# Layer 1 of a diffusion step: other turns at the passage into it, and another order of weights, gate and tiles at its end

## The chip, the cores and the metric

The kernel runs on one core of a Trainium2 chip. The metric is the device time of one launch in microseconds (us), median of several runs. The engines named are TensorE (PE; PEld is its weight load), VectorE (DVE), ScalarE (ACT), GpSimd (POOL) and SyncE (SP). SP and POOL issue nearly all DMAs, each through a queue of its own.

## The reference, cut to what matters

There are 640 tokens (512 of the sample, 128 of the context, which is the fifth tile of 128 tokens and is modulated by rows of its own), a model width of 1024 and two layers. Layer 0 is attention with a gated MLP beside it, layer 1 is centred pooling; each is followed by a squared-ReLU MLP of width 4096. All arithmetic that counts is float32.

```python
def squared_relu_mlp(h, w1, w2):
    a = jax.nn.relu(h @ w1)
    return (a * a) @ w2

# pooling mixer of layer 1: group g has the window w of (2, 4, 8, 16)
mean = (cs[:, end, sl] - cs[:, start, sl]) / cnt          # centred mean over w tokens
outs.append((mean - h32[..., sl]) @ w_pool[gi])

# every sub-layer: RMSNorm -> shift, scale -> mixer or MLP -> gate -> residual add
# at the end: y = rms_norm(x, final_g)
```

## The kernel before, in words

**Products.** A float32 product is made of three fast ones (fp32r): each operand is split into a high and a low part, and lines 823, 824 and 825 issue high by high, high by low, and low by high. For a weight the high part is a copy on ScalarE (L213). Its low part is made in one of two ways: VectorE subtracts the high part from the raw weight (L223, "VectorE makes the low part"), or ScalarE writes the negative high part (L216) and a GpSimd DMA adds the raw weight to it from memory (L220). In both cases L825, or L824 where the weight is the moving operand, has to wait for the low part.

**The stream of weights.** `st` holds a list of items, one for each piece of a weight, in the order in which they are used. `st.pump(n)` takes the next n: it issues loads on SP while raw tiles are free, and writes ScalarE's copy; the low part by VectorE is put into `lag` and written at once (`lows()`), except while `st.lagging` is set: then it is written at the next `pump` or `need`. `st.need(key)` pumps until a weight is there. `st.lo = None` selects the way over ScalarE and the DMA. So the places of `pump` in the program decide where a weight's passes stand in the engines' queues.

**MLP.** The 640 tokens go in two chunks (columns) of 320, or 328 and 312 in layer 0. In `mlp`, block b of 512 of the 4096 inner columns has four up tiles (`up_ps`, over eight parts of h, `h0` to `h7`) and then the down product (`dn_ps`). The square-ReLU of an up tile is L1502 to L1506: VectorE (`r`), ScalarE, VectorE (`aa`). In layer 0's last two blocks the down products of the second chunk are added to x for d = 0 to 7; `per_d0` squares each result for the norm.

**The passage from layer 0 to layer 1.** When seven eighths of the second chunk are done, `tick0` calls `pool_mm(0, …)`: the pooling's product for the first chunk, its residual adds (L1429), squares (L714, L729), the sum over partitions (`R_ps`, L740), an rsqrt on 128x3 values (L663 to L668, tile nrm5), its spread over the columns (L684) and then h (generator `g0`: L766 on VectorE, L770 on ScalarE, L774 on VectorE for each of eight parts). Between the squares `pool_mm` pumps a weight of block 0 of layer 1, `w1(1,0,·)`. The second chunk's pooling (generator `g1`: products `pt` L1903, `hh` L1907, windows `win` L1945, differences `dif` L1981) is interleaved with this. The string table `TURNS` says in what order, one entry at each up tile: '0' a step of g0, '1' a step of g1, 'w' a weight by ScalarE and the DMA, 'W' a weight by VectorE.

**The end.** Layer 1's last block has two more up tiles that are made with seven products of sums instead of eight (`up7`, `product`: L1632 u2, u3, r on VectorE). The output is computed with tokens as rows: tile t of 128 tokens, half q of 512 columns, in the order `LASTS = 4, 3, 2, 0, 1` (4 is the context). The sum over the earlier blocks, y, is multiplied by the gate's row (L2032; G for the context is row 1, for the others row 0), x is added to it by a GpSimd DMA from `xT` (L2033), and the last block's product comes in by gy = ps·G (L2042) and y + gy (L2043). Then follow the product with final_g (L2059), the rsqrt and the output. The context's tile takes another way: its last product is added to y first (L1738), and then the gate is applied. Row 0 of the gate is loaded by SP (L2020) just ahead of the last `up7`, row 1 and final_g behind it.

Of the kernel before, what the change touches and what calls it, by code (L numbers as in the profile page):

```python
# [45 lines left out]
H512 = slice(0, 512)  # L46
TAIL = slice(0, 256), slice(256, 512)
PARKS = 0, 1, 4, 3, 2
PARK_AT = {(0, 4): 1, (0, 5): 1, (0, 6): 1, (0, 7): 1, (1, 4): 1, (1, 5): 2, (1, 6): 2, (1, 7): 1}
# [5 lines left out]
STEPS = (4,) * 8  # L55
TURNS = '11w', 'w', '10', 'w01', '0w1', '01110', '11W11', '1', 'w0101', 'w1', '', '1', '', '11111', '111', '', '0w'
VM_LAG = 3, 4
# [74 lines left out]
class Weights:  # L132
# [3 lines left out]
    def __init__(self, nc, raw):  # L136
        self.nc, self.raw = nc, raw
        self.items, self.loaded, self.done = [], 0, 0
        self.raw_live, self.raw_cap, self.tiles, self.of = 0, RAWB, {}, {}
        self.raws = {}  # L140
        self.slots = None
        self.caps = {}

        self.lo = nc.vector
        self.own = {}
        self.hold = None
        self.slow = ()
        self.later, self.skip = [], False
        self.keep, self.second = {}, None
        self.lag, self.lagging = [], False  # L150
# [40 lines left out]
    def pump(self, n=1):  # L191
# [4 lines left out]
        while n > 0 and self.done < len(self.items):  # L196
# [9 lines left out]
            if use is None:  # L206
                if own is None:
                    self.of[key], w = self.slots.take([128, 2, 1024], F32R)
                else:
                    w = own()  # L210
                r = ts[0][:, 0:size]
                hi, lo = w[:, 0, 0:size], w[:, 1, 0:size]
                self.nc.scalar.activation(out=hi, in_=r, func=AF.Copy)  # L213
                eng = None if key[0] in self.slow else self.lo
                if eng is None:
                    self.nc.scalar.activation(out=lo, in_=hi.bitcast(F32), func=AF.Copy, scale=-1.0)  # L216
                    src, shape = loads[0]
                    if len(shape) == 2:
                        lo = lo.rearrange("p (k n) -> p k n", k=shape[0])
                    self.nc.gpsimd.dma_start(out=lo, in_=src, accum_op=ALU.add)  # L220
                else:
                    self.lag.append(
                        lambda: eng.tensor_tensor(out=lo, in0=r, in1=hi.bitcast(F32), op=ALU.subtract)  # L223
                    )
                self.tiles[key] = w
                rest = None
            else:
                rest = use(ts)
# [58 lines left out]
def body(ctx, tc, a):  # L287
# [303 lines left out]
    def add_w1s(l, b):  # L591
        for p in range(FB // 2):
            src = [(rows(a["w_ff1"][l], k, 4, b * 512 + p * 256, 256), (4, 256)) for k in (0, 4)]
            for i in range(7):
                key = ("w1s", l, b, p, i)
                st.add(key, [] if i else src, 0, w1s_use(l, b, p, i))
                st.keep[key] = 2 if i == 6 else 0

    def add_w2h(l, b):
        for i in range(4):  # L600
            for k, h in [(i // 2 * 2, i % 2) if b == NFB - 1 else (i % 2 * 2, i // 2)]:
                st.add(("w2", l, b, k, h), [(rows(a["w_ff2"][l], b * FB + k, 2, h * 512, 512), (2, 512))], 1024)

    def add_w2(l, b):
        for k in range(FB):
            r = (b * FB + k) * 128
            st.add(("w2", l, b, k), [(a["w_ff2"][l, r:r + 128, :], (1024,))], 1024)

    add_w1(0, 0)
    vm = vmods(1)  # L610
    for b in range(1, NFB + 1):
        n0 = len(st.items)
        if b < NFB:
            add_w1(0, b)
        add_w2(0, b - 1)
        ws, st.items[n0:] = st.items[n0:], []
# [8 lines left out]
    for b in range(NFB):  # L625
        if b >= 2:
            add_w1s(1, b)
        add_w2h(1, b)

# [839 lines left out]
    def mlp(l, C, H, lead, CL, per_d, per_c, mid, tick=None, turn=None, seven=False):  # L1469
# [58 lines left out]
        def down(b, d, c, ps=None, last=True, ks=range(FB)):  # L1528
# [3 lines left out]
            for j, k in enumerate(ks):  # L1532
                if seven:
                    w, v = st.need(("w2", l, b, k - k % 2, d // 4)), k % 2 * 4 + d % 4
# [60 lines left out]
        def up7(b, p, last=False):  # L1595
            n = C[0][1]
            gates = [(t, q) for t in LASTS[1:] for q in range(2)] if last else []

# [53 lines left out]
            pd = product(1, 2, None, True)  # L1652
            st.pump()
            pb = product(2, 1, None, True)
# [29 lines left out]
        def blocks7(f0):  # L1684

            st.lagging = True
            for b in range(NFB):
                if b >= f0:
                    for p in range(FB // 2):
                        if b == NFB - 1 and p:  # L1690
                            gate_load(0, rawp.tile([128, 1024], F32, tag="raw", name="G"))
                        up7(b, p, b == NFB - 1 and p == 1)
# [27 lines left out]

                todo = [(t, q) for t in LASTS for q in range(2)]
                st.pump(4)
                early = cut(todo[0:4])
# [5 lines left out]
                zs += [st.slots.take([128, 2, 1024], F32)[1].rearrange("p a n -> p (a n)") for _ in range(2)]  # L1729
                cell["zs"] = [z[:, 0:1024] for z in zs]  # L1730
                for t, q in todo:
                    i = LASTS.index(t)
                    for v in TAIL if (t, q) == todo[-1] else (H512,):
                        ps = early.pop((t, q), None)
                        ps = down_t(b, t, q, v, ps, True, range(FB) if ps is None else (3, 2))
                        if not i:
                            y = tile_q(t, q)
                            vec.tensor_tensor(out=y, in0=cols(ps), in1=y, op=ALU.add)  # L1738
                            last_gate(t, (q,))
                        else:  # L1740
                            last_more(t, q, v, ps)
                            last_sq(t, q, v, q + (v.start > 0))
                    if q and i == 2:

                        for k in range(2):
                            last_sq(LASTS[0], k, H512, k)
                        last_out(LASTS[0:3], False)
                    elif q and i > 2:
                        last_out(LASTS[i:i + 1], i == 4)

# [73 lines left out]
        while f2 < NFB:  # L1824
# [10 lines left out]
            if tick and f2 == NFB - 2:  # L1835
                for c, sizes in zip(C, AHEAD):
                    d0 = 0
                    for n in sizes:
# [5 lines left out]
                        if c is C[1] and d0 + n == KD:  # L1844
                            for k in range(FB):
                                st.free(("w2", l, f2, k))
                        tick(c, d0)
                        for d in range(d0, d0 + n):
                            residual(down(f2 + 1, d, c, pss[d - d0]), d, c, modc[l, 5])
                            per_d(c, d)  # L1850
                        d0 += n
                    per_c(c)
                for k in range(FB):
                    st.free(("w2", l, f2 + 1, k))
                return
# [189 lines left out]
    def last_sq(t, q, v, i):  # L2045
# [3 lines left out]
        if (t, "ss") not in cell:  # L2049
            i3 = LASTS.index(t)  # L2050
            if ("ss", i3 // 3) not in cell:
# [9 lines left out]
    def last_out(ts, both):  # L2061
        i3, n = LASTS.index(ts[0]), len(ts)
        ss = cell["ss", i3 // 3]
# [18 lines left out]
    xT = dr.tile([T, D], F32, name="xT")  # L2082
    grow = dr.tile([2, D], F32, name="grow")
    LASTS = (4, 3, 2, 0, 1)

    def pool_mm(ci, N, gs=POOL_ORDER):
# [3 lines left out]
        for g in gs:  # L2090
            for m in range(2):
# [7 lines left out]
                N.square(2 * g + m)  # L2099
                if ci == 0 and m:  # L2100
                    st.pump()

# [10 lines left out]
    def tick0(c, d):  # L2113
# [7 lines left out]
        keep()  # L2121
        st.lo = None
        st.caps["w1", 1, 0, 0] = RAWB
        N[0] = Norm(x, C1[0], vec)
# [4 lines left out]
    def per_d0(c, d):  # L2129
# [5 lines left out]
        if c == C0[1]:  # L2135
            bg.step(3)
            if d >= POOL_AT:
                st.pump()

# [15 lines left out]
    def turn1(what):  # L2155


        for t in what:
            if t in "01":
                next((g0, g1)[int(t)], None)  # L2160
            else:
                st.lo = None if t == "w" else vec
                st.pump()
                st.lo = vec

    turn1(TURNS[0])

# [103 lines left out]
```

## Time and profile before

| | us |
|---|---|
| median of 3 runs | 1283.76 (1283.36 to 1283.88) |
| the profiled execution | 1285.38 |
| its span (first to last instruction) | 1283.6 |
| TensorE matmul busy | 1247.0 (97%) |
| TensorE weight load busy | 1135.7 (88%) |
| VectorE busy | 796.9 (62%) |
| ScalarE busy | 571.1 (44%) |
| GpSimd busy | 198.5 (15%) |

The mean granted TensorE clock of the profiled execution is 0.988 of 2.4 GHz. Waits, rows and clocks below are from this one execution; its time is 1.6 us above the median. Each row of an instruction has its start, its duration, engine, line, operation, output<-input, and in brackets the idle time of its engine just before it and what ended it.

### The profile page before, as it was taken

How to read it: one execution, taken by the hardware profiler on the slowest of the kernel's cores; microseconds unless marked ns; L12 is line 12 of the kernel's file. 1: busy time of each engine (PE TensorE's matmuls, PEld its weight loads, DVE VectorE, ACT ScalarE, POOL GpSimd, SP SyncE). 2: the span in 40 equal slices, each digit the busy share in tenths (PEclk: the TensorE clock that was granted, in tenths of full speed). 3: DMA queues.
4: the chain of work that ended last, by engine and by line, in shares of the span. 5: the costliest groups of instructions: out<-in, count | busy, mean ns of one | idle time of the engine just before them, and what ended most of it. 6: DMA issues, size and time to landing. Idle time of an engine off the chain costs nothing. (4 is left out here: it accounts for less than half of the span.)

```text
span 1283.6 us, 19571 instructions
## 1 busy us (share of the span) xinstructions
PE 1247.0 (97%) x7744; PEld 1135.7 (88%) x7744; DVE 796.9 (62%) x1455; ACT 571.1 (44%) x1022; POOL 198.5 (15%) x181
## 2 busy tenths in 40 slices
PE   6999999999999999999999999899999999999986
PEld 4899975689999999999999999889898989989875
DVE  5753854554766566666666637775576556675667
ACT  4445654543554434334332424745444515445154
POOL 0010122212122221313131314210000000000030
PEclk9999999999999999999999999899999999999988
DMA  7752696250344443535353441904113343132273
GB/s 297 262 167 68 152 254 235 97 197 1 120 139 139 124 154 119 158 121 159 120 161 118 142 139 29 234 27 128 60 33 100 83 82 96 37 122 76 66 128 102
DMA packets 79163, 161.89 MB, mean 126 GB/s; under 512 B 7728, under 2 KB 34864, under 8 KB 78560
## 3 DMA queue, kind: packets, MB, share of 16 engines
q1 hardware_dynamic: 69296, 145.94, 35.6%
q0 software_dynamic: 9344, 14.35, 6.2%
q8 instruction: 61, 1.00, 0.3%
q10 hardware_dynamic: 432, 0.35, 0.1%
q14 instruction: 30, 0.25, 0.1%
HBM read 149.46 MB, written 8.02 MB: 123 GB/s over the span
## 5 line engine op out<-in xcount | busy, mean ns | idle before, releaser
L823 PE MATMUL up_ps<-h,w 128*128 128x320 f32 (+2 forms) x800 | 251.8, 315 | 4.7 <-DVE r L1632 3.1
L824 PE MATMUL up_ps<-h,w 128*128 128x320 f32 (+2 forms) x800 | 249.4, 312 | 1.2 <-DVE h L774 1.2
L825 PE MATMUL up_ps<-h,w 128*128 128x320 f32 (+2 forms) x800 | 249.9, 312 | 0.0
L213 ACT ACTIVATE w<-raw 128x1024 fp32r<-128x1024 f32 (+4 forms) x131 | 132.8, 1027 | 109.6 <-DMA raw<-w_ff 84.1
L223 DVE TENSOR_TENSOR w<-raw,w 128x1024 fp32r<-128x1024 f32 (+4 forms) x122 | 151.5, 1249 | 48.0 <-ACT w L213 47.1
L823 PEld LDWEIGHTS up_ps<-h,w 128*128 128x128 f32 x800 | 152.4, 190 | 9.1 <-issue 6.7
L823 PE MATMUL dn_ps<-aa,w 128*128 128x328 f32 (+1 forms) x512 | 159.1, 311 | 0.0
L824 PE MATMUL dn_ps<-aa,w 128*128 128x328 f32 (+1 forms) x512 | 159.0, 311 | 0.0
L825 PE MATMUL dn_ps<-aa,w 128*128 128x328 f32 (+1 forms) x512 | 158.1, 309 | 0.0
L824 PEld LDWEIGHTS up_ps<-h,w 128*128 128x128 f32 x800 | 152.7, 191 | 1.9 <-DVE h L774 1.6
L825 PEld LDWEIGHTS up_ps<-h,w 128*128 128x128 f32 x800 | 152.2, 190 | 0.3 <-DMA w<-w_ff 0.3
L484 POOL TENSOR_TENSOR acc<-acc,raw 128x1024 f32<-128x1024 f32 x42 | 100.7, 2397 | 303.7 <-ACT raw L482 303.7
L824 PE MATMUL dn_ps<-w,aa 128*128 128x512 f32 (+1 forms) x324 | 126.1, 389 | 2.4 <-DVE w L223 2.4
L823 PE MATMUL dn_ps<-w,aa 128*128 128x512 f32 (+1 forms) x324 | 126.8, 391 | 0.0
L825 PE MATMUL dn_ps<-w,aa 128*128 128x512 f32 (+1 forms) x324 | 126.3, 390 | 0.0
L1429 DVE SCALAR_TENSOR_TENSOR x<-dn_ps,mod,x 128x328 f32<-128x328 f32 (+2 forms) x168 | 67.3, 435 | 68.0 <-PE dn_ps L825 67.3
L576 ACT ACTIVATE w<-raw 128x512 fp32r<-128x512 f32 x84 | 51.0, 625 | 120.5 <-DVE raw L583 120.5
L823 PEld LDWEIGHTS dn_ps<-aa,w 128*128 128x128 f32 x512 | 96.4, 188 | 1.8 <-ACT r L1502 0.8
L825 PEld LDWEIGHTS dn_ps<-aa,w 128*128 128x128 f32 x512 | 96.3, 188 | 0.0
L824 PEld LDWEIGHTS dn_ps<-aa,w 128*128 128x128 f32 x512 | 96.2, 188 | 0.1
L482 ACT ACTIVATE raw<-raw,cs 128x1024 f32<-128x1024 f32 x42 | 48.3, 1150 | 62.5 <-DVE acc L477 58.0
L824 PEld LDWEIGHTS dn_ps<-w,aa 128*128 128x128 f32 x324 | 61.3, 189 | 15.5 <-DVE w L223 2.8
(403 smaller groups left out, 2421.1 us busy)
## 6 DMA issues: line engine op xcount, KB each, us to landing
raw<-w_ff SPq DMA_DIRECT2D x126, 512.0 KB, 3.8
raw<-w_mod SPq DMA_DIRECT2D x80, 512.0 KB, 3.9
raw<-w_m SPq DMA_DIRECT2D x16, 512.0 KB, 6.5
raw<-w_out SPq DMA_DIRECT2D x8, 512.0 KB, 4.5
w<-w_ff POOLq DMA_DIRECT2D x8, 512.0 KB, 9.8
kT<-ckvT POOLq DMA_DIRECT2D x4, 768.0 KB, 11.0
xr<-x SPq DMA_DIRECT2D x5, 512.0 KB, 6.2
xs<-x SPq DMA_DIRECT2D x2, 1280.0 KB, 10.1
```

The costliest lines, as they stand in the source:

```text
L213: self.nc.scalar.activation(out=hi, in_=r, func=AF.Copy)
L223: lambda: eng.tensor_tensor(out=lo, in0=r, in1=hi.bitcast(F32), op=ALU.subtract)
L482: act(out=raw if k else acc[1], in_=raw, func=AF.Copy, scale=w[1])
L484: nc.gpsimd.tensor_tensor(out=acc[1], in0=acc[1], in1=raw, op=ALU.add)
L576: act(out=w[:, 0], in_=src, func=AF.Copy)
L823: mm(ps, lhsT=st_[0], rhs=mv[0], start=first, stop=False, skip_group_check=on)
L824: mm(ps, lhsT=st_[0], rhs=mv[1], start=False, stop=False, skip_group_check=on)
L825: mm(ps, lhsT=st_[1], rhs=mv[0], start=False, stop=last, skip_group_check=on)
L1429: vec.scalar_tensor_tensor(out=xv, in0=ps[:, p0:p0 + c1 - c0], scalar=gate[:, d, m:m + 1], in1=xv, op0=ALU.mult, op1=ALU.add)
```

## The change

Five things are changed; the matmuls and their order on TensorE are the same.

1. The last two `w_ff2` blocks of layer 0 are loaded in halves (two k by 512 columns), so that half of their slots come free at d = 3. The four weights `w1(1,0,·)` are then made at d = 3, 4 and 5 in `per_d0`, and `pool_mm` no longer pumps.
2. `TURNS` is written anew: the first chunk's h (0) stands ahead, and one weight is made over ScalarE and the DMA ('w') and three by VectorE ('W'), where before there were four 'w' ahead of the first 'W'. `st.lagging` is set before the first turn instead of later.
3. Row 0 of the gate is an item of the weights' stream, and stays in its raw tile.
4. Two of the last block's `w_ff2` pieces have their low part made by ScalarE and the GpSimd DMA (`st.dma`) instead of by VectorE.
5. The order of tiles at the end is 3, 2, 4, 0, 1 (`ENDS`); the gates of 3, 2 and 0 are applied during the last `up7`, those of 4 and 1 behind it, and tile 4 takes the same way as the others.

```diff
+ENDS = 3, 2, 4, 0, 1
-TURNS = '11w', 'w', '10', 'w01', '0w1', '01110', '11W11', '1', 'w0101', 'w1', '', '1', '', '11111', '111', '', '0w'
+TURNS = '11', '', '01', '0w', '01W', '0W1', '011', '0W1', '11', '11', '11', '11', '1', '11111', '111', '', '0w'
...
-                eng = None if key[0] in self.slow else self.lo
+                eng = None if key[0] in self.slow or key in self.dma else self.lo
...
-        add_w2(0, b - 1)
+        (add_w2h if b > NFB - 2 else add_w2)(0, b - 1)
...
+        if b == NFB - 1:
+            st.add(("gate",), [(grow[0:1, :].to_broadcast([128, D]), (D,))], 0, lambda ts: cell.update({("G", 0): ts[0]}))
+            st.keep["gate",] = 0
+            st.dma = [("w2", 1, b, 0, h) for h in range(2)]
         add_w2h(1, b)
...
-            gates = [(t, q) for t in LASTS[1:] for q in range(2)] if last else []
+            gates = [(t, q) for t in ENDS[0:2] + ENDS[3:4] for q in range(2)] if last else []
...
-            st.pump()
+            st.pump(1 + last)
...
-                        if b == NFB - 1 and p:
-                            gate_load(0, rawp.tile([128, 1024], F32, tag="raw", name="G"))
...
-                st.pump(4)
+                st.pump(5)
+                st.lows()
                 early = cut(todo[0:4])
...
+                last_gate(NT - 1)
+                last_gate(ENDS[-1])
...
-                        if not i:
-                            y = tile_q(t, q)
-                            vec.tensor_tensor(out=y, in0=cols(ps), in1=y, op=ALU.add)
-                            last_gate(t, (q,))
-                        else:
-                            last_more(t, q, v, ps)
-                            last_sq(t, q, v, q + (v.start > 0))
+                        last_more(t, q, v, ps)
+                        last_sq(t, q, v, q + (v.start > 0))
...
+                            if c is C[1] and d == 3:
+                                free2(f2, 0)
+                                free2(f2 + 1, 0)
...
                 N.square(2 * g + m)
-                if ci == 0 and m:
-                    st.pump()
...
-        st.lo = None
-        st.caps["w1", 1, 0, 0] = RAWB
+        st.caps["w1", 1, 0, 2] = RAWB
...
-            if d >= POOL_AT:
-                st.pump()
+            if 3 <= d < POOL_AT:
+                st.lo = None
+                st.pump(2 if d == 3 else 1)
...
+    st.lagging = True
     turn1(TURNS[0])
```

**VectorE's queue at the passage**, around the four square-ReLUs of layer 1's first block, before (numbers behind names are those of buffers; after the change all lines are one to ten higher):

```order
L1981 SCALAR_TENSOR_TENSOR dif2_8225<-win_8223,hh2_8014 128x2x328
L1945 TENSOR_TENSOR win_8241<-hh1_8018 128x2x330
L1503 TENSOR_TENSOR r_8244<-r_8244,up_ps_8052 128x320
L1506 TENSOR_TENSOR aa_8243<-r_8244,aa_8243 128x320
L1503 TENSOR_TENSOR r_8250<-r_8250,up_ps_8053 128x320
L1506 TENSOR_TENSOR aa_8249<-r_8250,aa_8249 128x320
L1945 TENSOR_TENSOR win_8255<-win_8241 128x2x328
L1503 TENSOR_TENSOR r_8258<-r_8258,up_ps_8054 128x320
L1506 TENSOR_TENSOR aa_8257<-r_8258,aa_8257 128x320
L1503 TENSOR_TENSOR r_8264<-r_8264,up_ps_8055 128x320
L1506 TENSOR_TENSOR aa_8263<-r_8264,aa_8263 128x320
L1980 TENSOR_TENSOR win_8255<-win_8255,cnt_3357 128x2x2x8
```

The same place after the change (here L224 is the low part of a weight, L1513 and L1516 the square-ReLU, L1947 a window):

```order
L1983 SCALAR_TENSOR_TENSOR dif2_8243<-win_8235,hh2_8014 128x2x328
L1947 TENSOR_TENSOR win_8247<-hh1_8018 128x2x330
L1513 TENSOR_TENSOR r_8250<-r_8250,up_ps_8044 128x320
L1516 TENSOR_TENSOR aa_8249<-r_8250,aa_8249 128x320
L1947 TENSOR_TENSOR win_8255<-win_8247 128x2x328
L1513 TENSOR_TENSOR r_8258<-r_8258,up_ps_8045 128x320
L1516 TENSOR_TENSOR aa_8257<-r_8258,aa_8257 128x320
L224 TENSOR_TENSOR w_8183<-raw_8083,w_8183 128x1024
L1982 TENSOR_TENSOR win_8255<-win_8255,cnt_3358 128x2x2x8
```

Behind the fourth square-ReLU now stands the low part of w_8183, the third that VectorE makes there; the two others stand further ahead in the queue. TensorE reads w_8183 in the first up tile of block 1.

**GpSimd's queue at the end**, before, the first six of ten alike (x0 and x1 are the two halves of x's columns):

```order
L2033 DMA x0_2778<-xT_3359 128x4x128
L2033 DMA x1_2779<-xT_3359 128x4x128
L2033 DMA x0_2778<-xT_3359 128x4x128
L2033 DMA x1_2779<-xT_3359 128x4x128
L2033 DMA x0_2778<-xT_3359 128x4x128
L2033 DMA x1_2779<-xT_3359 128x4x128
```

After:

```order
L2035 DMA x0_2779<-xT_3360 128x4x128
L2035 DMA x1_2780<-xT_3360 128x4x128
L221 DMA w_11709<-w_ff2 128x2x512
L2035 DMA x0_2779<-xT_3360 128x4x128
L2035 DMA x1_2780<-xT_3360 128x4x128
L221 DMA w_11731<-w_ff2 128x2x512
L2035 DMA x0_2779<-xT_3360 128x4x128
```

Two weights' low parts (L221 adds the raw weight from memory) now stand between the transfers of x, behind those of the first and of the second tile.

**VectorE's queue at the last product of the last `up7`**, before (L581 is the low part of a sum of weights, L2032 a gate, r the row for which a product waits):

```order
L581 TENSOR_TENSOR w_11629<-raw_11384,w_11629 128x512
L1632 TENSOR_TENSOR u2_11701<-p1_11671,up_ps_11688 128x320
L1632 TENSOR_TENSOR u3_11702<-u2_11701,up_ps_11673 128x320
L2032 TENSOR_TENSOR x0_2778<-x0_2778,G_11652 128x4x128
L2032 TENSOR_TENSOR x1_2779<-x1_2779,G_11652 128x4x128
L581 TENSOR_TENSOR w_11629<-raw_11386,w_11629 128x512
L1632 TENSOR_TENSOR r_11657<-u3_11702,up_ps_11714 128x320
```

After:

```order
L582 TENSOR_TENSOR w_11626<-raw_11381,w_11626 128x512
L582 TENSOR_TENSOR w_11626<-raw_11383,w_11626 128x512
L1642 TENSOR_TENSOR u2_11701<-p1_11666,up_ps_11688 128x320
L1642 TENSOR_TENSOR u3_11702<-u2_11701,up_ps_11668 128x320
L2034 TENSOR_TENSOR x0_2779<-x0_2779,raw_11388 128x4x128
L2034 TENSOR_TENSOR x1_2780<-x1_2780,raw_11388 128x4x128
L1642 TENSOR_TENSOR r_11652<-u3_11702,up_ps_11713 128x320
```

The gate reads raw_11388, the raw tile of the stream's gate item, instead of the tile G of a load of its own, and the second L582 has moved ahead of the sums.

## Rows read from the trace of the kernel before

**Rows 1.** Window of the end: start:end, length, busy (count) by engine, clock, DMA, GB/s.
```profile
1200.00:1284.00 84.00, 66.63 (x341) 59.15 (x339) 54.17 (x103) 34.16 (x74) 13.06 (x10) 0.88 0.46 101
```
**Rows 2.** TensorE's waits, whole span: for whom, us in all, times, longest.
```profile
PE up_ps L823 <- DVE r L1632: 3.1, 1, 3.1
...
PE dn_ps L824 <- DVE w L223: 2.4, 1, 2.4
...
PE R_ps L740 <- DVE sq L729: 1.5, 1, 1.5
PE R_ps L684 <- DVE nrm5y L668: 1.4, 1, 1.4
PE up_ps L824 <- DVE h L774: 1.2, 2, 0.9
...
PE up_ps L823 <- DVE r L1503: 0.7, 1, 0.7
```
**Rows 3.** Windows of half clock behind these places, columns as in rows 1.
```profile
810.20:817.03 6.83, 6.83 (x29) 6.83 (x29) 3.85 (x13) 6.09 (x10) 1.47 (x2) 0.50 1.08 261
1233.46:1240.28 6.82, 6.19 (x23) 6.22 (x24) 6.82 (x12) 5.16 (x9) 6.82 (x6) 0.50 0.80 189
1250.52:1253.94 3.42, 3.42 (x10) 2.68 (x9) 1.38 (x2) 0.00 (x0) 0.00 (x0) 0.50 1.29 160
```
**Rows 4.** Timeline of TensorE at the passage: the matmul that reads the third weight's low part.
```profile
833.12 0.41 PE L825 MATMUL up_ps<-h,w 128*128 128x320 f32 x1
```
**Rows 5.** Timeline of ScalarE before and at the passage: idle time, one weight's pass.
```profile
787.88 0.46 ACT L714 ACTIVATE sq<-x 128x312 f32<-128x312 f32 x1 [8.29 <-DVE x L1429]
...
795.11 1.04 ACT L213 ACTIVATE w<-raw 128x1024 fp32r<-128x1024 f32 x1
```
**Rows 6.** VectorE at the passage: two rows of rsqrt, one window, its waits in it.
```profile
806.00 0.18 DVE L665 RECIPROCAL nrm5y<-nrm5y 128x3 f32<-128x3 f32 x1 [0.60 <-ACT nrm5y L664]
806.21 1.73 DVE L666 TENSOR_TENSOR nrm5t<-nrm5y,nrm5v 128x3 f32<-128x3 f32 x1
...
809.37:837.42 28.05, 27.09 (x164) 26.39 (x164) 20.39 (x46) 22.42 (x43) 4.81 (x4) 0.88 0.88 201
...
DVE h L774 <- ACT h L770: 3.7, 3, 2.4
DVE aa L1506 <- ACT aa L1505: 2.2, 4, 0.5
DVE ht L766 <- ACT hh L1907: 1.1, 1, 1.1
```
**Rows 7.** Timeline of VectorE behind the passage: a weight's low part and its next row.
```profile
875.58 1.23 DVE L223 TENSOR_TENSOR w<-raw,w 128x1024 fp32r<-128x1024 f32 x1 [0.46 <-ACT w L213]
876.72 0.48 DVE L1503 TENSOR_TENSOR r<-r,up_ps 128x320 f32<-128x320 f32 x1
```
**Rows 8.** GpSimd's DMAs: weights at 780:840 (first), x at 1220:1284 (second), x's issues.
```profile
DMA to landing us min/median/max: 6.2/9.8/11.2
...
DMA to landing us min/median/max: 4.6/10.6/11.7
...
1232.96 10.47 POOL L2033 DMA_DIRECT2D x<-xT  x8 [380.77 <-DVE x L2032]
```
**Rows 9.** Timeline of TensorE at the end: the product that waits, the second matrix's start.
```profile
1234.09 0.60 PE L823 MATMUL up_ps<-h,w 128*128 128x320 f32 x1 [3.11 <-DVE r L1632]
...
1240.47 0.40 PE L823 MATMUL dn_ps<-w,aa 128*128 128x512 f32 x1
...
1242.08 0.39 PE L824 MATMUL dn_ps<-w,aa 128*128 128x512 f32 x1
```
**Rows 10.** Timeline of VectorE at the end: the first gate, the first gy, the fourth.
```profile
1231.64 1.29 DVE L2032 TENSOR_TENSOR x<-x,G 128x512 f32<-128x512 f32 x2 [2.81 <-DMA G<-grow]
...
1254.51 0.69 DVE L2042 TENSOR_TENSOR gy<-dn_ps,G 128x512 f32<-128x512 f32 x1 [0.79 <-PE dn_ps L825]
...
1261.43 0.69 DVE L2042 TENSOR_TENSOR gy<-dn_ps,G 128x512 f32<-128x512 f32 x1 [0.57 <-PE dn_ps L825]
```

More of the change, by code (lines that the diff above doesn't have):

```diff
@@ L146, in __init__ @@
         self.hold = None
-        self.slow = ()
+        self.slow, self.dma = (), ()
         self.later, self.skip = [], False
@@ L597, in add_w1s @@
                 st.keep[key] = 2 if i == 6 else 0
+    halves = set()
     def add_w2h(l, b):
+        halves.add((l, b))
         for i in range(4):
@@ L607, in add_w2 @@
             st.add(("w2", l, b, k), [(a["w_ff2"][l, r:r + 128, :], (1024,))], 1024)
+    grow = dr.tile([2, D], F32, name="grow")
     add_w1(0, 0)
@@ L1532, in down @@
             for j, k in enumerate(ks):
-                if seven:
+                if (l, b) in halves:
                     w, v = st.need(("w2", l, b, k - k % 2, d // 4)), k % 2 * 4 + d % 4
@@ L1719, in blocks7 @@
                     continue
-                todo = [(t, q) for t in LASTS for q in range(2)]
-                st.pump(4)
+                todo = [(t, q) for t in ENDS for q in range(2)]
+                st.pump(5)
+                st.lows()
                 early = cut(todo[0:4])
@@ L1730, in blocks7 @@
                 cell["zs"] = [z[:, 0:1024] for z in zs]
+                last_gate(NT - 1)
+                last_gate(ENDS[-1])
                 for t, q in todo:
-                    i = LASTS.index(t)
+                    i = ENDS.index(t)
                     for v in TAIL if (t, q) == todo[-1] else (H512,):
@@ L1735, in blocks7 @@
                         ps = down_t(b, t, q, v, ps, True, range(FB) if ps is None else (3, 2))
-                        if not i:
-                            y = tile_q(t, q)
-                            vec.tensor_tensor(out=y, in0=cols(ps), in1=y, op=ALU.add)
-                            last_gate(t, (q,))
-                        else:
-                            last_more(t, q, v, ps)
-                            last_sq(t, q, v, q + (v.start > 0))
[L1743 to L1749, printed above, removed]
+                        last_more(t, q, v, ps)
+                        last_sq(t, q, v, q + (v.start > 0))
+                    if q and i >= 2:
+                        last_out(ENDS[0:3] if i == 2 else ENDS[i:i + 1], i == 4)
         spare = []
@@ L1844, in mlp @@
                         if c is C[1] and d0 + n == KD:
-                            for k in range(FB):
-                                st.free(("w2", l, f2, k))
+                            free2(f2, 1)
                         tick(c, d0)
@@ L1852, in mlp @@
                     per_c(c)
-                for k in range(FB):
-                    st.free(("w2", l, f2 + 1, k))
+                free2(f2 + 1, 1)
                 return
@@ L2049, in last_sq @@
         if (t, "ss") not in cell:
-            i3 = LASTS.index(t)
+            i3 = ENDS.index(t)
             if ("ss", i3 // 3) not in cell:
@@ L2061, in last_out @@
     def last_out(ts, both):
-        i3, n = LASTS.index(ts[0]), len(ts)
+        i3, n = ENDS.index(ts[0]), len(ts)
         ss = cell["ss", i3 // 3]
@@ L2082, in body @@
     xT = dr.tile([T, D], F32, name="xT")
-    grow = dr.tile([2, D], F32, name="grow")
     LASTS = (4, 3, 2, 0, 1)
```

## The prediction

> **What bounds the kernel now.** TensorE is busy for 97% of the span (the page's first part, in the table above), so the kernel is as long as TensorE's matmuls, its waits, and the stretches in which it runs at half clock. I read the views in this order. First the slices of the page and the window of the end [rows 1]: TensorE loses its time at the passage from layer 0 to layer 1, near 800, and at the end, where it is busy 66.6 of 84 us at a mean clock of 0.88. Second its waits [rows 2]: the long ones are all on VectorE. At the end they are 3.1 us (a product of the last block, for VectorE's subtraction r) and 2.4 us (the second matrix, for a weight's low part). At the passage they are 1.5 us (sum of squares), 1.4 us (the rsqrt's row) and 0.9 us (an h). Third the clock [rows 3]: 1.2 GHz instead of 2.4 behind each of these places, for 6.8, 6.8 and 3.4 us, which costs half of that: 3.4, 3.4 and 1.7 us. So 9.3 us of waits and 8.5 us of half clock lie where the change works, and it can win at most some 18 us. Whether it wins them is decided by what VectorE and the GpSimd DMA queue have to do before TensorE may go on, so fourth came VectorE's rows and waits [rows 6], and fifth the times from issue to landing [rows 8].
>
> **The passage, TensorE's gains.** Four weights w1(1,0,·) are made by ScalarE and an accumulating DMA. Before, their eight ScalarE passes of 1.04 us [rows 5], 8.4 us in all, lie among the squares of the norm. After, they are issued while layer 0's last residuals run, where ScalarE is idle for 8.29 us [rows 5]: cost nothing, the idle time covers it. Without them the squares are paced by VectorE's additions; I take 0.6 of the 1.5 us before the sum of squares [rows 2] as won (an estimate; the rest is VectorE's). The rsqrt chain then no longer meets a busy ScalarE: its 0.60 us wait goes, and so does about 1.0 of the 1.73 us that a 128x3 product took there [rows 6] (the 128x3 reciprocal ahead of it took 0.18). So the row's spread comes 0.6 + 0.6 + 1.0 = 2.2 us earlier. With shorter waits the half clock behind them (3.4) goes, and since the first chunk's h now leads, the 0.9 us wait for h [rows 2]; I allow 0.4 us for new handoffs. TensorE would then stand at the matmul that is at 833.12 before [rows 4] by 833.1 - (2.2 + 3.4 + 0.9 - 0.4) = 827.0.
>
> **The passage, what that matmul waits for.** This matmul (block 1's first, chunk 0, part k = 6 of h, third product) reads the low part of weight w_8183. Before, ScalarE and the DMA make it well ahead. After, it is the third weight that VectorE makes, and since the lag is switched on before the first turn, its subtraction is written only at the next pump: the order above shows it behind all four square-ReLUs and the five windows, on VectorE's own queue. Before, VectorE gets through that same work (the ht and h, the second rsqrt, the products pt, windows, four square-ReLUs) from 809.37 to 837.42, 28.05 us, 20.39 of them busy [rows 6]. After, it starts 2.2 us earlier, at 807.2; two low parts stand in between, each worth 1.14 us (875.58 to 876.72 [rows 7]); ScalarE has fewer passes there, of whose waits I take 0.5 us off; and the third low part itself takes 1.23 us [rows 7]. 807.2 + 28.05 + 2.28 - 0.5 + 1.23 = 838.2. TensorE, there at 827.0, waits some 11 us for it and goes on at 838.2 instead of 833.1: **+5.1 us**. No wait of this kind is in the trace of before, so it has ends: if every wait of VectorE for ScalarE's h and hh goes (3.7 + 1.1 [rows 6]; the four handoffs of 0.5 stay), where I took 0.5 off, it is 4.3 us less, +0.8; if none goes and each of the three low parts waits 0.46 for ScalarE as the one at 875.58 did [rows 7], +7.0. I stay near the upper half, since VectorE's h waits for ScalarE's half of the same h in a chain, which fewer weights shorten little.
> Behind a wait of 3.1 us TensorE's clock fell for 6.8 us and behind one of 2.4 us for 3.4 us [rows 2, 3]; an idle stretch of 11 us is longer than both, so I add **+2.5** (1.7 to 3.4). After it VectorE has its square-ReLUs behind it, and the 0.7 us wait for r [rows 2] goes: **-0.7**. The passage is +5.1 + 2.5 - 0.7 = **+6.9** (from 0.8 + 1.7 - 0.7 = +1.8 to 7.0 + 3.4 = +10.4).
>
> **The end.** The gate row G0 now comes with the weights' stream, long before it is used, so VectorE's 2.81 us wait for it [rows 10] goes, and with it TensorE's 3.11 us and the half clock from 1234.09 [rows 9] to 1240.28 [rows 3], worth half of 6.2, 3.1. One more low part (L581) now stands ahead of the sum, 0.5. So the second matrix's first matmul could start at 1240.47 - 3.1 - 3.1 + 0.5 = 1234.8 [rows 9].
> But it needs the low part of w2(1,7,0,0), and its second group that of w2(1,7,0,1), and these two are now made by GpSimd's accumulating DMA. In GpSimd's queue the first stands behind the transfers x of tile 3, the second behind those of tile 2 too. VectorE's first gate starts 2.81 us earlier and 0.5 later, at 1229.3, so the first x is issued at 1230.1; eight issues took 10.47 us [rows 8], 1.31 each, so the two weights are issued at 1232.7 and 1236.5. The accumulating weights at the passage took 6.2 to 11.2 us to land, median 9.8; the x transfers of this very queue 4.6 to 11.7, median 10.6 [rows 8]. With 9.8 they land at 1242.5 and 1246.3. After the second come 18 matmuls (0.23 each: the first and the eighth start at 1240.47 and 1242.08 [rows 9]; so 4.1), about 2.4 of half clock (between 1.7 and 3.1), and six for the rest of the first output, 1.4: VectorE's first gy at 1254.2, not at 1254.51 [rows 10]: -0.3. So a wait of about 1234.8 to 1242.5 takes the place of the 3.11 us, another the place of the 2.42 us, and nothing is won.
> From there VectorE sets the end: it runs without a break to the last output. The context's tile, which before had only its product with final_g left there, now passes gy and the addition in that stretch too: for each half an operation like the 0.69 of gy [rows 10] and a second of the same size, 2 x (0.69 + 0.69), with their handoffs 2.9 us; one wait of 0.57 [rows 10] goes. +2.3. The end is -0.3 + 2.3 = **+2.0**. With a landing of 6.2 it is 3.6 less, -1.6; with 11.7 and 3.4 of half clock 2.9 more, +4.9.
> What a page says against this price: the Trainium skill, page "DMA: Bandwidth & Descriptors", section "Anatomy of one DMA — SWDGE (gpsimd) path", fits 2.0 us plus bytes/436e3, which is an estimate of 3.2 us for 512 KB; the trace disagrees with 6.2 to 11.2 us [rows 8]. By the page the second weight would land at 1239.7, 6.6 us earlier, and with 0.7 less of half clock the end would be about -5.3, and the whole +1.6, 1285.4. I hold to the rows.
> The six gates instead of eight in the last block, the halves of layer 0's last two w_ff2 blocks and the earlier freeing of their slots cost nothing on the path: TensorE's order is unchanged and the same matmuls read the same bytes.
>
> **Sum.** +6.9 + 2.0 = +8.9. The sum is of differences within the profiled execution (1285.38, span 1283.6), which is 1.6 above the median of the runs shown; set against that median, 1283.76 + 8.9 = 1292.7.
>
> **Rivals.**
> A, faster: VectorE reaches the third low part before TensorE wants it. It decides at 833.1, the matmul's time before. If it is there at 827.0, the passage is -6.1 - 0.7 = -6.8, and with the end's +2.0 the whole is -4.8: 1279.0. For it speaks only that 7.7 us of VectorE's 28.05 are idle; against it, that even without any wait for ScalarE the walk ends at 833.9.
> B, no change: all of VectorE's waits for ScalarE go, half clock is at its least (+1.8), and the queue delivers as at its best, 6.2 us (-1.6): +0.2, 1284.0. The page's rule ends near this too.
> C, slower still: no wait of VectorE goes, half clock at its most, both DMAs at 11.7: +10.4 + 4.9 = +15.3, 1299.1.
> D: that the change doesn't do what it says. Its rows show that G0 and the weights do move, so I give it no chance of its own.
>
> **How the numbers follow.** Forecast 64% (about 1287 to 1297), A 7%, B 13%, C 16%. The range 1285 to 1298 leaves out A, half of B and the upper part of C, just under 2 in 10. A measurement of this kernel tells 0.2% (2.6 us) from no change. Faster by more: A and a little of B, 0.08. Within it: most of B, 0.10. Slower: the rest, 0.82.
>
> **What would show it.** At the passage of the changed kernel: the sum of squares waits under 1 us, no half clock at once behind it, and one long TensorE wait on "VectorE w" at a third product of up_ps, some 11 us, with half clock behind it. If that wait is under 5 us, the step on VectorE's queue is wrong, and A or B holds. At the end: no wait for r at a product, two waits of dn_ps on the GpSimd DMA of w_ff2, together over 8 us, and VectorE without a break from the first gy on. If these DMAs land in under 7 us, the price of the queue is wrong.

## The result and the profile after

The changed kernel takes 1293.03 us in the median of 4 runs (1290.36 to 1294.83), the kernel before 1283.82 (1283.36 to 1285.01). The ratio is 1.0069, with a 95% interval of 1.005 to 1.0088: slower by 6 to 11 us. Forecast were 1292.7 and 8.9 us more. The profiled execution took 1293.31, with a span of 1291.4 against 1283.6.

TensorE's waits in the whole span of the changed kernel (for whom; us in all, times, longest), to be read against [rows 2]:

```profile
PE dn_ps L834 <- DMA w<-w_ff: 10.8, 2, 8.2
PE up_ps L835 <- DVE w L224: 7.8, 1, 7.8
...
PE up_ps L833 <- DVE u L1642: 1.8, 6, 0.8
...
PE R_ps L750 <- DVE sq L739: 0.6, 1, 0.6
```

All the waits that the change aimed at are gone or short: 3.1 (r at the end), 2.4 (low part by VectorE), 1.4 (rsqrt's row) and 0.9 (h) are not in the list any more, 1.5 has become 0.6. In their place stand two that were not there: 7.8 us for a low part by VectorE, and 8.2 and 2.6 us for low parts by the GpSimd DMA (10.8 in the list). Both kinds are a low part that stands too far back in a queue.

The stretches of half clock in the changed kernel, columns as in [rows 1], against [rows 3]:

```profile
806.14:816.38 10.24, 10.24 (x45) 10.24 (x44) 7.61 (x21) 5.30 (x10) 0.32 (x4) 0.50 0.40 75
833.45:843.69 10.24, 4.61 (x18) 4.57 (x19) 9.07 (x16) 2.41 (x5) 0.10 (x1) 0.50 0.22 73
1243.05:1256.70 13.65, 6.23 (x14) 4.51 (x15) 4.03 (x6) 0.29 (x1) 7.32 (x6) 0.50 1.33 190
```

Each new wait has half clock in it and behind it. The matmuls under half clock behind the 7.8 us wait are those from 839.08 on, so 4.6 of the second stretch's 10.24 us count, and cost 2.3.

Where the time went is read from the same matmul in both traces. Three such pairs on TensorE's timeline (before, then after, each time): the second chunk's down product ahead of the passage, a down product behind it, and an up product ahead of the end:

```profile
786.14 0.30 PE L823 MATMUL dn_ps<-aa,w 128*128 128x312 f32 x1
892.90 0.39 PE L824 MATMUL dn_ps<-w,aa 128*128 128x512 f32 x1
1224.95 0.31 PE L825 MATMUL up_ps<-room,w 128*128 128x320 f32 x1
```
```profile
786.80 0.30 PE L833 MATMUL dn_ps<-aa,w 128*128 128x312 f32 x1
898.48 0.39 PE L834 MATMUL dn_ps<-w,aa 128*128 128x512 f32 x1
1229.25 0.31 PE L835 MATMUL up_ps<-room,w 128*128 128x320 f32 x1
```

The changed kernel is 0.7 us behind ahead of the passage (TensorE does the same work up to there; in other runs below this offset is between -0.5 and 4.0, so spans of single executions must not be compared without it). It is 5.6 behind after the passage, 4.3 at 1225, and 7.8 at the end of the span. So the passage cost 4.9 us, 1.3 of them came back on the way, and the end cost 3.5. The matmuls are the same in number and shape throughout; in the end, by the new order of tiles, they stand for other tokens than before.

The rows of the changed kernel that answer to those of the prediction, first TensorE's timeline ([rows 4, 9]), then VectorE's ([rows 6, 7, 10]):

```profile
839.08 0.64 PE L835 MATMUL up_ps<-h,w 128*128 128x320 f32 x1 [7.80 <-DVE w L224]
...
1239.24 0.40 PE L833 MATMUL dn_ps<-w,aa 128*128 128x512 f32 x1
...
1247.88 0.77 PE L834 MATMUL dn_ps<-w,aa 128*128 128x512 f32 x1 [8.24 <-DMA w<-w_ff]
...
1253.37 0.76 PE L834 MATMUL dn_ps<-w,aa 128*128 128x512 f32 x1 [2.59 <-DMA w<-w_ff]
```
```profile
805.66 0.16 DVE L676 TENSOR_TENSOR nrm5t<-nrm5y,nrm5v 128x3 f32<-128x3 f32 x1
...
837.81 1.22 DVE L224 TENSOR_TENSOR w<-raw,w 128x1024 fp32r<-128x1024 f32 x1
...
1260.43 0.69 DVE L2044 TENSOR_TENSOR gy<-dn_ps,raw 128x512 f32<-128x512 f32 x1 [13.02 <-PE dn_ps L835]
...
1286.92 0.49 DVE L2077 TENSOR_SCALAR w<-w,ry1y 128x512 f32<-128x512 f32 x1
```

VectorE's third low part runs from 837.81 to 839.03, and TensorE's matmul starts at 839.08: it was the last thing that the matmul waited for. At the end TensorE starts the second matrix at 1239.24; its second matmul already needs the first low part, and stands for 8.24 us.

### The profile page after: what moved, and what is told of

Read it like the earlier page. It is cut to its first block, busy times and chain, and to the rows that moved or that the text cites. A ratio compares the mean times of both kernels' runs of the same rounds, so it can differ in the third digit from the quotient of the medians.

```text
span 1291.4 us, 19563 instructions
## 1 busy us (share of the span) xinstructions
PE 1246.6 (97%) x7744; PEld 1137.8 (88%) x7744; DVE 797.5 (62%) x1458; ACT 571.6 (44%) x1021; POOL 197.7 (15%) x180
## 4 chain that ended last, share of the span: by engine, by line
PE 81%; DVE 8%; ACT 6%; DMA 3%; issue 2%; POOL 0%; ACTq 0%; DVEq 0%; POOLq 0%
PE dn_ps L834 11%; PE dn_ps L833 11%; PE dn_ps L835 11%; PE up_ps L833 9%; PE up_ps L835 8%; PE up_ps L834 8%; PE o_ps L1334 1%; PE wo_ps L833 1%; PE wo_ps L834 1%; PE wo_ps L835 1%; DVE w L582 1%; PE mod_ps L363 1%; PE t_ps L1301 1%; DMA w<-w_ff 1%; PE s_ps L833 1%
## 5 line engine op out<-in xcount | busy, mean ns | idle before, releaser
L224 DVE TENSOR_TENSOR w<-raw,w 128x1024 fp32r<-128x1024 f32 (+4 forms) x123 | 152.6, 1248 | 46.3 <-ACT w L214 45.1
L834 PE MATMUL dn_ps<-w,aa 128*128 128x512 f32 (+1 forms) x324 | 126.7, 391 | 10.8 <-DMA w<-w_ff 10.8
## 6 DMA issues: line engine op xcount, KB each, us to landing
w<-w_ff POOLq DMA_DIRECT2D x7, 512.0 KB, 11.3
```

Of the source, the lines that this page charges most:

```text
L834: mm(ps, lhsT=st_[0], rhs=mv[1], start=False, stop=False, skip_group_check=on)
```

## The experiments

All ratios are to the kernel before on the same chip, with 95% intervals; on these chips the kernel before has medians of 1284.7 to 1285.2, with single runs from 1281.3 to 1289.6. "By the matmuls" means the difference between matched matmuls as above, so without the offset ahead of the passage. What the end costs or gains "by the spans" is the span's difference less the offset at 1225. Both compare single executions with the one profiled execution of before.

**Each half of the change alone (e1, e2).** First the passage's part (halves, early weights, `TURNS`, lag) with the old end, then the end's part (gate item, `st.dma`, `ENDS`) with the old passage.

> Only the passage's part of the change (w_ff2 halves, four weights made early, new turns, lag on before the first turn); the end is the kernel before's. Theory (passage and end each cost, and add up): the 7.8 us wait of TensorE for the third low part is there, and half clock around it, so by the times of the same matmuls in the two traces +4.3 us: 1288; the end's waits of 3.1 and 2.4 us as before. Rival (the passage's loss is given back by a later wait that is shorter when TensorE comes late): 1284 to 1285.

> Only the end's part of the change (gate row in the weights' stream, two low parts by the GpSimd DMA, tile order 3, 2, 4, 0, 1); the passage is the kernel before's. Theory: the 3.1 us wait goes, but two waits of the second matrix for the GpSimd DMA, 8 and 2.6 us, come, and VectorE's tail is 2.0 longer: +3.5, 1287.3. Rival (the end loses only because the passage makes it late, or its gain from the gate row outweighs): 1281 to 1284.

Measured: 1.002 (1.0008 to 1.0032) for the passage, +2.6 us; 1.0049 (1.0035 to 1.0063) for the end, +6.3 us. Together 1.0069, what the whole change gave: the halves add up. The waits of each stand in its own trace; in the first

```profile
PE up_ps L828 <- DVE w L223: 10.5, 1, 10.5
PE up_ps L826 <- DVE r L1635: 3.2, 1, 3.2
PE dn_ps L827 <- DVE w L223: 2.4, 1, 2.4
```

and in the second

```profile
PE dn_ps L831 <- DMA w<-w_ff: 10.7, 2, 8.0
```

The passage cost less than I expected (2.6, not 4.3), and the end more (6.3, not 3.5). In the passage-only run, half clock at 806 is not there; TensorE comes to the low part earlier and waits 10.5 us in place of 7.8, for a moment on VectorE that lies 1.0 us earlier when the offset ahead of the passage is taken off. By the matmuls this passage cost 3.6 to the matmul at 893, and 2.4 to 1225. In part the end differs because the old end was slow in the profiled execution of before: by the spans the same old end is 1.9 us shorter in this first run, where half clock stands from 1236.65 to 1240.06, not for 6.8 us [rows 3]. Set against that, the changed end costs 6.1 us in the second run.

**The third low part, written at once (e3).**

```diff
-TURNS = '11', '', '01', '0w', '01W', '0W1', '011', '0W1', '11', '11', ...
+TURNS = '11', '', '01', '0w', '01W', '0W1', '011', '0W1', 'L11', '11', ...
...
-            if t in "01":
+            if t == "L":
+                st.lows()
+            elif t in "01":
```

> The changed kernel with one difference: the third weight's low part is written on VectorE's queue right at the next turn, ahead of the windows and the square-ReLUs, not behind them. Theory (the place on VectorE's queue makes the 7.8 us wait): that wait is gone or under 1 us. VectorE still has the same work, so TensorE meets it later, at the second chunk's pooling, for the square-ReLU's r, with 3 to 5 us: 3 to 5 us better than the changed kernel, 1288 to 1290. Rival (the clock decides: half clock starts at 806, before the wait, and stays): under 1.5 us better, 1291.5 to 1293.

Measured: 1.0032 (1.0013 to 1.005), 1290.27 us; by the ratios that is 4.7 us better than the changed kernel's 1.0069. VectorE now makes that low part at 827.1, and the wait is gone. But at the second chunk's pooling TensorE waits for VectorE (waits between 825 and 870):

```profile
PE pool_ps L2095 <- DVE r L1513: 3.0, 2, 2.0
PE up_ps L833 <- DVE r L1513: 1.0, 1, 1.0
PE R_ps L694 <- DVE nrm6y L678: 0.7, 1, 0.7
```

So the place in VectorE's queue made the wait, and 4 of the 7.8 us only move on to where VectorE's work is wanted next. The rival (the clock decides) falls: half clock stands there too, from 807 on, 6.8 us in two stretches, and another 6.8 us stand behind the new waits, from 861.71. The profiled execution is the slowest of the nine, 3.0 us above their median; by the matmuls its passage is 2.2 us better than the changed kernel's at 1225 (1.5 against 3.6).

**The end's two low parts by VectorE (e4).** One line is taken out of the changed kernel:

```diff
-            st.dma = [("w2", 1, b, 0, h) for h in range(2)]
```

> The changed kernel with one difference: the two low parts of the last w_ff2 block are made by VectorE again, not by the GpSimd DMA. Theory (these DMAs stand behind x transfers in GpSimd's queue and set the second matrix): both waits, 8.2 and 2.6 us, go, at most 2 us for VectorE come instead, and the first gy comes 5 to 7 us earlier: 1286 to 1288. Rival (the tail behind is set by the x transfers' landing or by VectorE, whatever the weights do): within 2 us of the changed kernel, 1291 to 1293.

Measured: 0.9955 (0.9937 to 0.9972), 1279.47 us: 1.1% better than the changed kernel, and faster than the kernel before. This is twice what I expected. TensorE has no wait above 0.8 us left in the end, and no half clock there; the window from 1225 to 1262 (columns as in [rows 1]) and VectorE's first gy are

```profile
1225.00:1262.00 37.00, 36.20 (x189) 31.79 (x188) 32.54 (x58) 20.28 (x43) 12.95 (x10) 1.00 0.75 129
...
1246.61 0.69 DVE L2043 TENSOR_TENSOR gy<-dn_ps,raw 128x512 f32<-128x512 f32 x1
```

The gy comes 13.8 us earlier than in the changed kernel, of which 1.4 lie ahead of the end: the 10.8 us of the waits themselves go, and the half clock around them with them. By the spans the end is 9.0 us shorter than before, and 12.5 shorter than the changed kernel's. VectorE makes the two low parts between the gates at 1.22 us each, and TensorE never has to wait for them. So the end without the DMAs wins what it was built for: the 3.1 and 2.4 us waits of before and the half clock behind both.

**The weights ahead of x in GpSimd's queue (e7).** Still by DMA, but no gate is applied in the last `up7`; all ten follow behind the weights.

```diff
-            gates = [(t, q) for t in ENDS[0:2] + ENDS[3:4] for q in range(2)] if last else []
+            gates = []
...
-                last_gate(NT - 1)
-                last_gate(ENDS[-1])
+                for t in ENDS:
+                    last_gate(t)
```

> The changed kernel, still with two low parts by the GpSimd DMA, but all gates and so all transfers of x are written behind them, so that the weights lead GpSimd's queue. Theory (their place behind x makes them late): the two waits of the second matrix shrink from 8.2 and 2.6 us to at most 4 together, the weights land 5 to 9 us after their issue; the first gy waits for x instead, so the time may not fall. Rival (the accumulating DMA is slow by itself beside the loads): the waits stay above 8 us together, landings at 10 us and more.

Measured: 1.0029 (1.0014 to 1.0044). The weights' landings (min, median, max of the two), first with the weights ahead, then in the changed kernel:

```profile
DMA to landing us min/median/max: 5.5/7.8/10.1
```
```profile
DMA to landing us min/median/max: 11.3/12.9/14.5
```

The wait for the first is 0.25 us, for the second still 5.0. The first weight, alone in the queue, lands after 5.5 us; the second, issued 2.05 us later, just behind SP's loads of the gate's second row and of final_g, after 10.1. So the place behind x is about half of the price (10.8 us of waits become 5.3): neither theory nor rival alone. That the rest comes from SP's two loads beside it is read from these times and was not tried. Even at the head of its queue this DMA takes 5.5 us where VectorE takes 1.22.

**The gate row, and a low part written at once (e8, and again e11).** The kernel before with the gate item in the stream and one line more, `st.lows()` (old tile order and passage, all low parts by VectorE):

```diff
+            st.add(("gate",), [(grow[0:1, :].to_broadcast([128, D]), (D,))], 0, lambda ts: cell.update({("G", 0): ts[0]}))
+            st.keep["gate",] = 0
...
-            st.pump()
+            st.pump(1 + last)
...
-                            gate_load(0, rawp.tile([128, 1024], F32, tag="raw", name="G"))
...
-                st.pump(4)
+                st.pump(5)
+                st.lows()
```

> The kernel before with the gate row in the weights' stream and nothing else of the change: tile order, way of the context's tile, low parts by VectorE and passage as before. Theory (the gate row is the end's gain, and the context's tile in third place makes VectorE's tail 2 us longer): no wait of 3.1 us, and 1 to 3 us better than the same with the new tile order: 0.991 to 0.993 of the kernel before. Rival (the new order gains too, by work for VectorE while TensorE fills the tail): worse than that one, 0.995 to 0.997.

> The kernel before with the gate row in the weights' stream alone, again, beside the two other kernels on the same chip: 0.993 to 0.997 of the kernel before by the first measurement. Theory and rival as for the two other runs: the passage's turns are worth 1 to 2 us against this, or nothing.

Measured: 0.9951 (0.9935 to 0.9967) and, on another chip, 0.9928 (0.991 to 0.9945). Both waits of the end are gone: the longest that TensorE has left between 1225 and 1262 is

```profile
PE up_ps L828 <- ACT w L213: 0.8, 1, 0.8
```

But the run is not the gate row alone, which its expectation takes it to be. `lagging` is on in the last blocks, so before, the last piece's low part was written only when a product asked for it, behind an addition that itself waits for TensorE's first output of the end. `st.lows()` writes it ahead of that addition. VectorE's rows before, then in e8:

```profile
1247.49 0.69 DVE L1738 TENSOR_TENSOR x<-dn_ps,x 128x512 f32<-128x512 f32 x1 [4.13 <-PE dn_ps L825]
1248.22 0.69 DVE L2032 TENSOR_TENSOR x<-x,w 128x512 f32<-128x512 f32 x1
1248.83 1.22 DVE L223 TENSOR_TENSOR w<-raw,w 128x1024 fp32r<-128x1024 f32 x1
```
```profile
1242.59 1.22 DVE L223 TENSOR_TENSOR w<-raw,w 128x1024 fp32r<-128x1024 f32 x1
1244.18 0.69 DVE L1742 TENSOR_TENSOR x<-dn_ps,x 128x512 f32<-128x512 f32 x1 [0.37 <-PE dn_ps L830]
...
1246.90 0.69 DVE L2046 TENSOR_TENSOR gy<-dn_ps,raw 128x512 f32<-128x512 f32 x1
```

TensorE's 2.42 us wait for a low part before ends at 1250.10, just behind the L223 of the upper rows. So by these rows the gate row removes the 3.1 us wait and `st.lows()` the 2.4 us one; with half of the 3.4 us of half clock behind it, that line is worth some 4.1 us (an estimate from [rows 2, 3]). No run has one without the other.

The first gy of e8 comes as early as with the new tile order, and both halves of the context's tile are by then past their last product. By the spans the end gains 10.0 us here and 9.0 with the new order (e4): about 1 us for the context's way through VectorE's tail, in single executions.

**Undoing the passage, or mending it, with the good end (e5, e6).** The first takes the changed end without `st.dma` and the old passage, the second the changed kernel without `st.dma` and with 'L'.

> The kernel before's passage with the changed end, whose two low parts VectorE makes. Theory (passage and end add up): the end is as in the run with VectorE's low parts, where no wait of the second matrix was left, and the passage's loss of 2.6 us by its matmuls is gone: 0.993 to 0.994 of the kernel before. Rival (the passage's loss was given back anyway, so undoing it gains nothing): 0.995 to 0.996, as that run.

> The changed kernel with both edits: the third low part written at once, and the end's low parts by VectorE. Theory (the passage's loss only moves to the second chunk's pooling): within 2 us of the run that has the end's edit alone, 0.994 to 0.996 of the kernel before. Rival (the third low part's place is the whole loss of the passage): 4 us better than that run, 0.992.

Measured: 0.9959 (0.9944 to 0.9974) and 0.9939 (0.9923 to 0.9955); with the changed passage as it is, 0.9955 (above). The old passage should have been 2.6 us better than that by the first experiment, and was not; the intervals are some 2 us to each side, so the times do not decide it. The matched matmuls say more: by 1225 the old passage stands between 0 and +1.4 us in its five profiled executions (before, e2, e5, e8, e11), the changed one between +2.4 and +3.6 in its four (after, e1, e4, e7), and the mended one at -0.8 and -0.7 in e6 and e9, at +1.5 in e3. So the changed passage does cost some 2 us against the old one. The mended passage is 2.0 us better by the ratios than the one with the wait, between what theory and rival expected, and 3.4 by the matmuls (e6 against e4), nearer to the rival. Its waits between 825 and 870 are again VectorE's:

```profile
PE up_ps L832 <- DVE r L1512: 2.1, 1, 2.1
PE pool_ps L2094 <- DVE r L1512: 1.6, 2, 1.0
```

**The best of both, and other turns (e9, e10).** The mended passage with the end of e8; then the same with turns in which the DMA makes three of block 1's low parts and VectorE one.

```diff
-TURNS = '11', '', '01', '0w', '01W', '0W1', '011', '0W1', 'L11', '11', ...
+TURNS = '11', 'w', '01', '0w', '01', '0w1', '01', '0W1', 'L1111', '11', ...
```

> The changed kernel's passage with the third low part written at once, and at the end only the gate row in the weights' stream (tile order, the context's way and VectorE's low parts as before). Theory (with the third low part in its place the new turns win a little: -0.8 us by the matmuls, against +0.8 to +1.3 of the old passage; the old tile order is 1.2 us shorter at the tail): 0.991 to 0.993 of the kernel before, 1 to 2 us better than the gate row alone. Rival (the passage is VectorE's work either way): equal to the gate row alone, 0.994 to 0.996.

> As the run before this, but with other turns: of the four weights of block 1 the first three are made by ScalarE and the DMA, only the fourth by VectorE, and two more steps of the second chunk's pooling come ahead. Theory (VectorE's work sets the passage, so two low parts less, 2.3 us, come back): no or shorter waits for r at the second chunk's pooling, but a wait of 2 to 4 us for a DMA's low part at block 1; together 0 to 2 us better, 0.990 to 0.993. Rival (the DMAs land too late, 10 us and more after issue): 2 us worse or more, 0.994 to 0.997.

Measured, on one chip with e11 (0.9928): 0.9921 (0.9904 to 0.9939) and 0.9914 (0.9893 to 0.9935), 1275.4 and 1275.2 us. Both beat both kernels, the one before by 9 to 11 us. Against e11 they are 0.9 and 1.8 us better by the ratios and 0.4 and 0.6 by the medians, which the intervals do not separate; by the matmuls to 1225, in single executions, 1.4 and 2.5. In the last, the DMA's low parts cost TensorE 0.4 us, and waits for r of 1.5 and 2.3 us stay.

## Why the prediction was right, and where its steps were not

The forecast, its sign and its mechanism hold: +9.2 us by the medians against +8.9. The terms, in the profiled execution, are less exact than their sum: the passage +3.6 by 1225 where +6.9 was forecast, the end +3.5 to 3.6 where +2.0 was. One error is 3.3 us too high, the other 1.5 too low, so that the whole came within 0.3 us of the medians is in part luck; by the matmuls and spans the whole is +7.1.

**The gains ahead of the low part.** The sum of squares came 0.9 us earlier (0.6 forecast), the row's spread 2.05 (2.2): the 128x3 product fell from 1.73 to 0.16 us, and the 0.9 us wait for h is gone. That product takes 1.67 to 1.74 us in all five executions of the old passage and 0.16 in all eight of the new ones; what in the weights' work held it was not tried. Half clock did not go: it stood from 806.14 to 816.38, and cost 5.1 us where I had taken 3.4 as won. With the same instructions up to there, three other runs (e1, e4, e7) have none at that place. So this step failed in this execution, and the runs show no cause for it that the program sets.

**The wait.** That half clock made only 1.0 us of difference here, for VectorE and not TensorE sets the moment. Forecast was 838.2, that is 838.9 with the offset of 0.7; it was 839.08. In the three executions without that half clock (e1, e4, e7) the moment comes some 0.75 us ahead of the forecast, in e4 with its offset of 0.2 at

```profile
837.69 0.64 PE L834 MATMUL up_ps<-h,w 128*128 128x320 f32 x1 [10.52 <-DVE w L224]
```

Only the wait's length differs more (7.8 us, 10.5 in the three others, 11 forecast), since TensorE comes earlier where it is not at half clock. This was the step on which the sign rested, and it was the order of VectorE's queue that gave it. That it was met so closely is partly luck, for the terms inside the walk were wrong. Of the 4.8 us in which VectorE waited for ScalarE's h and hh I took 0.5 off, arguing that these waits would stay; VectorE's waits from 807 to 840 in the changed kernel are

```profile
DVE r L1513 <- ACT r L1512: 2.0, 1, 2.0
DVE w L224 <- ACT w L214: 1.2, 1, 1.2
...
DVE h L784 <- ACT h L780: 0.6, 2, 0.4
```

So the waits for h all but went (in e4 1.2 us stay), and new ones for ScalarE's r and for a weight's high part, which I had not seen, took most of their place.

**After the wait.** Half clock cost 2.3 (2.5 forecast). The step that was mis-sized is what comes back: -0.7 was forecast, 2.5 by 893 was measured (the differences of the matched matmuls fall from 8.05 at 844 to 5.58). I counted only the 0.7 us wait for r, but the 0.7 us wait for the second chunk's rsqrt row, also in the list of before, goes too, and the remaining 1.1 us are in smaller steps. Another 1.3 come back between 893 and 1225 (below).

**The end.** TensorE at the second matrix at 1239.24 where 1234.8 and 4.3 of offset make 1239.1: the wait for r gone, as forecast. The two weights' landings were mis-sized: I took 9.8 us from the accumulating DMAs at the passage, and they took 11.25 and 14.5. GpSimd issues the next DMA 0.7 to 0.8 us after the last, not 1.31 as I took from eight in a row, so the second weight is issued 2 us earlier than forecast and stands longer in the queue. In this trace the queue's own pace sets the landing: the ten x and the two weights land in the order of issue, an x 1.4 to 1.5 us behind the one before it, a weight 2.5. First gy +1.6 where -0.3 was forecast; the tail from there on 26.49 us against 24.48, +2.0 (2.3 forecast). The fit of the Trainium skill, page "DMA: Bandwidth & Descriptors", section "Anatomy of one DMA — SWDGE (gpsimd) path", gives an estimate of 3.2 us for 512 KB. The traces disagree: 11.3 and 14.5 us, and 5.5 even for the weight that leads the queue (e7). The whole by that price, 1285.4, was not met.

**The rivals.** A (VectorE in time) did not happen; it takes one more letter in the table of turns (e3), and even then the passage gains little, since VectorE's work stays. B and C were not met: the landings were at and beyond C's end; VectorE's waits for h went, as in B, but others came. What I did not see is how much the end would win without the two DMAs: some 12 us, since with the waits the half clock goes.

## What to carry to other kernels

An operation that is taken off a busy engine must be priced by where it stands in the new queue, not by its own length: 1.22 us on VectorE became 8 us behind transfers that nobody was waiting for yet. Where work is written late (a lag, a list that is flushed at the next pump), count out in that engine's own rows what stands ahead of it and set it against the moment at which the reader is free; that moment came out within 0.2 to 0.8 us here, though the waits inside the walk did not. And a change of several parts is worth taking apart: two small parts of this one, the gate row in the stream and a low part written at once, made the kernel 0.5 to 0.7% faster, and another, the two low parts by DMA, took more than that away.

## What the runs showed of the hardware that I had not expected

**Half clock is not a function of the program alone.** Directly behind 803, ahead of the wait, the changed passage runs at half clock for 10.2 us in one execution, for 3.4 or 6.8 us in three (e3, e6, e9), and not at all in four others (e1, e4, e7, e10, the last with other turns); the old passage for 6.8 to 13.7 us. The mean granted clock of 24 executions of the kernel before on one chip lies between 0.983 and 0.992, and their times differ by up to 8 us. So comparisons of stages need matched instructions.

**The second matrix's matmuls are a little quicker behind the new passage.** Between 893 and 1225 the same matmuls (128x512) take a little less time, with no wait among them. Two groups of the lines' view, before and then after (count; busy us, mean ns):

```profile
L823 PE MATMUL dn_ps<-w,aa 128*128 128x512 f32 x279 | 109.3, 392 | 0.0
```
```profile
L833 PE MATMUL dn_ps<-w,aa 128*128 128x512 f32 x279 | 108.6, 389 | 0.0
```

From start to start, 835 such matmuls take 190.7 us before and 189.5 after: the 1.25 us that come back there, in every run with the changed passage and in none with the old one. The halves and their earlier release may put later weights into other slots; neither that nor that it is the cause was tried.
